# Hybrid encoder layer on one core: the Fourier group's fold as first work, raw column weights in memory of their own, residual squares to SBUF, output weights split before a scan unit

## The chip, the core and the metric

The kernel runs on one core of a Trainium2 chip. The core has a matrix engine (PE; its weight loads are listed as PEld), a vector engine (DVE), a scalar engine (ACT), a small general engine (POOL) and a sequencer that here issues nearly all DMA transfers (SP). Each takes its instructions in order from its own queue and waits on semaphores. SBUF is the working memory of 128 partitions; PSUM holds eight banks of 512 fp32 a partition, into which PE writes. The metric is the device time of one execution, in microseconds; the time before is the median of three runs.

## The reference: what is computed

One layer of a trunk over 2048 tokens of 1024 channels. A modulated RMS norm is followed by one input projection, whose columns go to a Fourier group and to a two-way gated linear attention group; both are gated, joined, projected back and added to the residual stream, and a last RMS norm follows.

```python
h = rmsnorm(x, norm_g[layer]) * (1.0 + scale[:, None, :]) + shift[:, None, :]
proj = h @ w_in[layer]
u_f, z_f, q, k, v, r, gf_low, gb_low = jnp.split(proj, pts, axis=-1)
y_f = fourier_mix(u_f, w_fmap[layer]) * jax.nn.silu(z_f)
y_g = gla_mix(q, k, v, gf_low, gb_low, w_af[layer], b_af[layer],
              w_ab[layer], b_ab[layer], gla_norm_g[layer]) * jax.nn.silu(r)
y = jnp.concatenate([y_f, y_g], axis=-1) @ w_out[layer]
x = x + gate[:, None, :] * y
...
# fourier_mix
spec = jnp.fft.fft2(ug, axes=(1, 3), norm="ortho").real
y = jnp.einsum("blgc,gcd->blgd", spec, w_map.astype(jnp.float32))
```

## The kernel before

**Halves and blocks.** The tokens are worked in two halves, the second (m = 1) first. For each half the normed input A is held in 14 SBUF tiles: seven combinations of quarter blocks, each as a high and a low part, since products are made of three matmuls (high by high, high by low, low by high), and a projection block of 2 x 2 quarters is made with seven products instead of eight. Column blocks (`block_col`, L272: q, k, z, r) take 84 matmuls of 512 columns; token blocks (`block_tok`, L315: u, v) take twice four times that in narrower ones. The weights of a block pass through `b_prep` for the second half: a raw tile is loaded, differences are formed on DVE (L228 to L236), ACT makes the high part (L48) and DVE the low one (L49), and the seven results, tiles named B in a pool of six, are stored for the first half, which only loads them.

**The start.** x of the second half is loaded (`x_tiles`), squared on ACT and summed on DVE (`x_rstd`: L138, L141, L142), summed over partitions on PE (L145), and the root is made on POOL (L148) and spread by PE (L164). Meanwhile PE makes the modulation rows from `ada` tiles, two tiles a row (L923 to L930). Then DVE scales x (L171) and A is built (L181 to L193, L48, L49).

**After the first value block.** `do_v(1, A, 0)` is followed by the loads of the fold and of the residual gate's weights, by `do_v(1, A, 1)`, by the fold, the gate row and the rows' squares. The fold multiplies the channel DFT table with each group's map: 32 matmul statements into eight PSUM tiles (L396), each copied by ACT to a staging tile (L399) and stored to `fold_d`. Its input tiles lie in the gate's pool. Then the token pools are closed and two column pools opened in their place, staging and `colraw`, the one raw tile for column weights; `do_q(1, A, 8)` is the first to use it.

**Scan and output.** A scan unit is one pair of heads over 256 tokens, done in two steps: a preparation on ACT and DVE (L493 to L543), scores (L553, L554), a product with the state (L603), a transpose (L564) and the state's update (L56, L575). Units are written beside projection blocks, which fill PE while ACT and DVE prepare. For the first half the last four column blocks, r, stand behind one unit each; then the first four pairs of output weights are loaded and split (`split_out_weights`, L1043, L1044) into the A tiles, which come free as the last block proceeds. The other four units stand beside Fourier parts of the output product (`out_fourier`, L843, 48 statements each), and the remaining splits are spread between them. At the end, for each 128 tokens, `out_fwd` adds the product to x and squares the sum for the norm (L872), with its unneeded result going back into the PSUM tile of the product.

**What sets the order.** The program text gives an order with priorities, and a list scheduler, which plans with a model of the machine, decides the queue of every engine. So a change of the text moves rows on all engines.

Of the kernel before, what the change touches and what calls it, by code (L numbers as in the profile page):

```python
# [12 lines left out]
F32 = mybir.dt.float32  # L13
F32R = mybir.dt.float32r
BF16 = mybir.dt.bfloat16
# [6 lines left out]
P = 128  # L22
# [13 lines left out]
def hybrid_kernel(ctx, tc, i, out):  # L36
# [4 lines left out]
    def load(dst, src):  # L41
        nc.sync.dma_start(dst, src)
# [336 lines left out]
            store(vd_[tt:tt + 2, :, cs].rearrange("a p n -> p a n"), v)  # L379
        block_tok(A, weights("tok", 2 + j, m), WC, 1, emit)  # L380

    def fold_load(gg, gw):
        fin = gw.tile([P, 2048], F32, tag="fold", name="fold_in", bufs=2)
        tabs = fin[:, 0:1024].rearrange("p (k w) -> p k w", k=2)
        wf = fin[:, 1024:2048].rearrange("p (g k d) -> p g k d", g=2, k=2)
        load(tabs, i["chtab"].rearrange("k p w -> p k w"))
        load(wf, i["w_fmap"][2 * gg:2 * gg + 2].rearrange("g (k p) d -> p g k d", p=P))
        return tabs, wf

    def fold(gg, tabs, wf):  # L390
        for g in range(2):
            for w in range(2):
                ps = pj_tile()
                for ct in range(2):
                    for k in range(2):
                        T.matmul(ps[:, ct * 256:(ct + 1) * 256], tabs[:, k, w * 256 + ct * P:w * 256 + (ct + 1) * P],  # L396
                                 wf[:, g, k, :], start=(k == 0), stop=(k == 1))
                s = stage_tile()
                S.activation(s[:, 0:512], ps[:], AF.Copy)  # L399
                store(fd_[:, 2 * gg + g, w * 512:(w + 1) * 512], s[:, 0:512])  # L400

    def gate_sums(gw):
        acc = gw.tile([P, D], F32, name="gacc")
# [392 lines left out]
    def tail_fwd(sc, os_, sr):  # L796
        for hp in range(2):
            o = os_[hp]
            ss = op.tile([P, 2], F32, tag="ss", name="ss", bufs=4)
            for h in range(2):  # L800
                jk = op.tile([P, 256], BF16, tag="jk", name="jk", bufs=1)
                S.activation(jk[:], o[:, h * 256:(h + 1) * 256], AF.Square, accum_out=ss[:, h:h + 1])  # L802
            r = rstd(ss[:], 2, 256)
            for h in range(2):
                V.tensor_scalar(o[:, h * 256:(h + 1) * 256], o[:, h * 256:(h + 1) * 256], r[:, h:h + 1], None,
                                ALU.mult)
            tp = pg.tile([P, 4, P], F32, tag="tr", name="otr")
            for c in range(4):
                T.transpose(tp[:, c, :], o[:, c * P:(c + 1) * P], ident[:])  # L809
            y = sr[:, 4 * hp:4 * hp + 4, :]  # L810
            V.tensor_tensor(y, tp[:], y, ALU.mult)
        return sr
# [50 lines left out]
    def out_fwd(sc, ys, yf):  # L863
# [5 lines left out]

        def residual(n):  # L870
            xs_ = gated_add(x, ps, n)
            S.activation(ps[n][:], xs_, AF.Square, accum_out=ss[:, n:n + 1])  # L872

        if sc == 15:
            for k in range(4):
# [20 lines left out]
    with ExitStack() as st_stack:  # L896
# [13 lines left out]
        def load_ada(j):  # L910
# [2 lines left out]
                load(t[h], i["w_ada"][j][:, 4 * h:4 * h + 4, :])  # L913
            return t

        xs = x_tiles(1)
        rb = x_rstd(xs)
        A = a_tiles()
        for j in range(KT):
# [17 lines left out]

    xstack.close()
    do_v(1, A, 0)
    gw = pool(glate, "gate")  # L940
    folds = [fold_load(g, gw) for g in range(2)]
    acc = gate_sums(gw)
    do_v(1, A, 1)
    for g in range(2):
        fold(g, *folds[g])
    gate_row(acc, gw)
    rows_rms(gw)
    tok.close()
    n_st = 2
    sp = pool(col, "stagec", side="right")  # L950
    cr = pool(col, "colraw", side="right")
    do_q(1, A, 8, qd_)
    do_q(1, A, 10, kd_)
    glate.close()
# [12 lines left out]
    for hp in range(2):  # L967
        store(sst_[hp], st_b[hp][:].rearrange("p h t -> p (h t)"))
    gstack.close()
    col.close()  # L970
    sp = pool(tok, "stage3", side="right")
    tk = pool(tok, "tokraw3", side="right")
# [93 lines left out]
            gts[blk] = gates(blk)  # L1066
        scan_back(blk, hp, gts[blk], st_b)

    for blk in range(12, 16):
        next_unit()  # L1070
        do_r(0, A, blk)
    for j in range(4):
        split_out_weights(j, st_w)
    ph2.close()
# [106 lines left out]
```

## Time and profile before

| what | us |
|---|---|
| median of three runs | 1695.24 |
| lowest, highest | 1693.71, 1698.9 |
| the profiled execution | 1696.42 |
| its span, from the first to the last instruction | 1694.6 |
| DMA moved in the span | 400.42 MB, mean 236 GB/s |

A page of the profile gives busy times of the engines, the span in 40 slices, the DMA queues, the chain of work that ended last, and groups of instructions by line with the idle time ahead of them. A row of the timeline has the start, the length, the engine (SPq is SP's issuing of transfers), the line, the operation, what it writes and reads, how many were merged, and in brackets how long the engine had been idle and what released it. A row of the stretches has the borders and length, for each engine the busy time and count, then the mean granted clock of PE, the DMA engines' busy share and the rate. An fp32 matmul statement stands in the profile as two records.

### The profile page before, as it was taken

The page shows a single profiled execution, that of the slowest core. Times are in us where ns is not written, and L with a number is a line of the kernel's source. Part 1 is how long each engine was busy: PE and PEld are TensorE (multiplying, and loading weights), DVE is VectorE, ACT ScalarE, POOL GpSimd, SP SyncE. Part 2 cuts the span into 40 slices and gives each one's busy share as a digit, 9 for nine tenths or more (in the row PEclk, how much of TensorE's full clock was granted, in tenths as well). Part 3 has the DMA queues.
Part 4 walks back from the last instruction along what each step waited for, and adds up shares of the span by engine and source line. Part 5 has one row for each costly group of instructions (what it writes and reads, how often), then busy time and mean ns, then how long its engine had stood idle before and what let it go on. Part 6 is the DMA issues. An engine that isn't in the chain of part 4 may idle for free. (4 is left out here: it accounts for less than half of the span.)

```text
span 1694.6 us, 25167 instructions
## 1 busy us (share of the span) xinstructions
PE 1580.2 (93%) x9012; PEld 1358.2 (80%) x9012; DVE 1174.1 (69%) x2424; ACT 692.9 (41%) x1294; POOL 60.8 (4%) x118
## 2 busy tenths in 40 slices
PE   5899899999989999999999999978999999999997
PEld 2599678778889988989998887857887778778876
DVE  4964588877578444887887646678876865777673
ACT  3723244433244201313232407677543543454452
POOL 0000000000000000000000000000010111111110
PEclk9999999999999999999999999978999999999999
DMA  8498888778977689879897688866654333343432
GB/s 293 161 389 325 294 317 288 278 281 307 327 286 284 226 267 363 277 234 319 252 337 220 224 289 277 286 225 226 222 165 145 122 130 119 115 137 127 149 94 75
DMA packets 220332, 400.42 MB, mean 236 GB/s; under 512 B 19504, under 2 KB 121776, under 8 KB 216624
## 3 DMA queue, kind: packets, MB, share of 16 engines
q1 hardware_dynamic: 220064, 398.56, 68.6%
q8 instruction: 71, 1.16, 0.3%
q14 instruction: 53, 0.43, 0.1%
q10 hardware_dynamic: 144, 0.26, 0.0%
HBM read 238.13 MB, written 160.63 MB: 235 GB/s over the span
## 5 line engine op out<-in xcount | busy, mean ns | idle before, releaser
L272 PE MATMUL pj<-A_hi,B 128*128 128x512 f32 x1344 | 437.0, 400 | 16.6 <-ACT B L48 12.8
L315 PE MATMUL pj<-B,A_hi 128*128 128x264 f32 (+1 forms) x1792 | 336.0, 288 | 17.5 <-DMA B<-btok_d 6.6
L272 PEld LDWEIGHTS pj<-A_hi,B 128*128 128x128 f32 x1344 | 251.2, 188 | 77.8 <-ACT B L48 15.1
L315 PEld LDWEIGHTS pj<-B,A_hi 128*128 128x128 f32 x1792 | 283.5, 193 | 22.1 <-DVE B L49 6.0
L272 PE MATMUL pj<-A_lo,B 128*128 128x512 f32 x672 | 267.4, 398 | 0.0
L315 PE MATMUL pj<-B,A_lo 128*128 128x264 f32 (+1 forms) x896 | 255.3, 287 | 2.3 <-DVE A_lo L49 2.3
L315 PEld LDWEIGHTS pj<-B,A_lo 128*128 128x128 f32 x896 | 173.0, 194 | 2.5 <-DVE A_lo L49 2.5
L272 PEld LDWEIGHTS pj<-A_lo,B 128*128 128x128 f32 x672 | 126.8, 189 | 27.1
L843 PE MATMUL po<-wo_hi,fhi 128*128 128x512 f32 x256 | 108.5, 424 | 12.1 <-ACT po L872 6.2
L843 PE MATMUL po<-wo_hi,ghi 128*128 128x512 f32 x256 | 103.9, 406 | 1.9 <-ACT ghi L48 1.9
L843 PE MATMUL po<-wo_lo,fhi 128*128 128x512 f32 x256 | 105.2, 411 | 0.0
L843 PE MATMUL po<-wo_lo,ghi 128*128 128x512 f32 x256 | 103.4, 404 | 0.0
L843 PE MATMUL po<-wo_hi,flo 128*128 128x512 f32 x256 | 95.2, 414 | 0.2 <-DVE flo L49 0.2
L843 PE MATMUL po<-wo_hi,glo 128*128 128x512 f32 x256 | 88.6, 410 | 2.6 <-DVE glo L49 2.6
L276 DVE TENSOR_TENSOR u<-u,pj 128x512 f32<-128x512 f32 x96 | 65.4, 681 | 26.0 <-PE pj L272 23.7
L583 ACT ACTIVATE vh<-v 128x512 fp32r<-128x512 f32 x64 | 40.1, 626 | 99.0 <-PE upd L56 87.2
L48 ACT ACTIVATE B<-raw 128x512 fp32r<-128x512 f32 x72 | 42.8, 624 | 91.2 <-DMA raw<-in_w_in 42.0
L575 DVE SCALAR_TENSOR_TENSOR state<-state,sm,upd 128x256 f32<-128x256 f32 x112 | 48.8, 474 | 37.0 <-PE upd L56 36.8
L320 DVE TENSOR_TENSOR u<-u,pj 128x264 f32<-128x264 f32 (+1 forms) x96 | 48.9, 515 | 35.8 <-PE pj L315 35.7
L843 PEld LDWEIGHTS po<-wo_hi,fhi 128*128 128x128 f32 x256 | 50.7, 198 | 25.8 <-ACT po L872 8.2
L56 PE MATMUL mapA<-PQ,wm 128*128 128x256 f32 x480 | 65.8, 287 | 1.8 <-ACT PQ L48 1.4
L56 PEld LDWEIGHTS mapA<-PQ,wm 128*128 128x128 f32 x480 | 62.4, 194 | 3.7 <-ACT PQ L48 1.9
(221 smaller groups left out, 3042.9 us busy)
## 6 DMA issues: line engine op xcount, KB each, us to landing
bcol_d<-B SPq DMA_DIRECT2D x84, 512.0 KB, 4.1
B<-bcol_d SPq DMA_DIRECT2D x84, 512.0 KB, 4.9
v<-v_d SPq DMA_DIRECT2D x64, 256.0 KB, 3.5
btok_d<-B SPq DMA_DIRECT2D x28, 528.0 KB, 9.2
B<-btok_d SPq DMA_DIRECT2D x28, 528.0 KB, 6.7
btok_d<-B SPq DMA_DIRECT2D x28, 512.0 KB, 4.5
B<-btok_d SPq DMA_DIRECT2D x28, 512.0 KB, 5.9
raw<-in_w_in SPq DMA_DIRECT2D x12, 1024.0 KB, 7.6
```

The lines of the kernel that those rows point to most:

```text
L48: S.activation(hi, src, AF.Copy)
L56: T.matmul(ps, a, b, start=(k == 0), stop=(k == n - 1))
L272: T.matmul(ps[:], B[k][0][:, bq, p, :], A[k][aq][:, p, :], start=(p == 0 and q == 0), stop=(p == 3 and q == 2))
L276: V.tensor_tensor(o, a, ps[:], ALU.add)
L315: T.matmul(ps[:, j, :], A[k][aq][:, p, t * P:(t + 1) * P], B[k][p // 2][:, bq, p % 2, :], start=(p == 0 and q == 0), stop=(p == 3 and q == 2))
L320: V.tensor_tensor(o[:, cut], a[:, cut], ps, ALU.add)
L575: V.scalar_tensor_tensor(state[:, h, :], state[:, h, :], dec[:, g:g + 1], up_[:, h, :], ALU.mult, ALU.add)
L583: S.activation(vh[:], v[:], AF.Copy)
L843: T.matmul(ps[n][:], a, wo[j0 + j][q][:, cs], start=(first and a is yh and q == 0), stop=(last and a is yl))
```

## The change

Four things are changed.

- The fold becomes the first work of the program: its tables and all four groups' maps are loaded ahead of x, into two tiles of the token weights' raw pool, and its matmuls are written ahead of `x_rstd`.
- `colraw` is opened right behind the first value block, in memory of its own on the left side, and closed after the scan's first part.
- The residual squares of `out_fwd` go to a scratch tile in SBUF, bf16, which the normalisation in `tail_fwd` shares (its tile grows from 256 to 512 columns).
- The fourth scan unit of the first half leaves the loop over the r blocks: three units stand with three r blocks, the fourth r block and the split of the first output weights follow, and then five units (instead of four) stand beside Fourier parts of the output.

```diff
--- before.py
+++ after.py
@@ -379,16 +379,15 @@
             store(vd_[tt:tt + 2, :, cs].rearrange("a p n -> p a n"), v)
         block_tok(A, weights("tok", 2 + j, m), WC, 1, emit)
 
-    def fold_load(gg, gw):
-        fin = gw.tile([P, 2048], F32, tag="fold", name="fold_in", bufs=2)
-        tabs = fin[:, 0:1024].rearrange("p (k w) -> p k w", k=2)
-        wf = fin[:, 1024:2048].rearrange("p (g k d) -> p g k d", g=2, k=2)
+    def fold_load():
+        tabs = tk.tile([P, 2 * BW], F32, tag="traw", name="fold_t", bufs=2)[:, 0:1024].rearrange("p (k w) -> p k w", k=2)
         load(tabs, i["chtab"].rearrange("k p w -> p k w"))
-        load(wf, i["w_fmap"][2 * gg:2 * gg + 2].rearrange("g (k p) d -> p g k d", p=P))
+        wf = tk.tile([P, 2 * BW], F32, tag="traw", name="fold_w", bufs=2)[:, 0:2048].rearrange("p (g k d) -> p g k d", g=4, k=2)
+        load(wf, i["w_fmap"].rearrange("g (k p) d -> p g k d", p=P))
         return tabs, wf
 
-    def fold(gg, tabs, wf):
-        for g in range(2):
+    def fold(tabs, wf):
+        for g in range(NG):
             for w in range(2):
                 ps = pj_tile()
                 for ct in range(2):
@@ -397,7 +396,7 @@
                                  wf[:, g, k, :], start=(k == 0), stop=(k == 1))
                 s = stage_tile()
                 S.activation(s[:, 0:512], ps[:], AF.Copy)
-                store(fd_[:, 2 * gg + g, w * 512:(w + 1) * 512], s[:, 0:512])
+                store(fd_[:, g, w * 512:(w + 1) * 512], s[:, 0:512])
 
     def gate_sums(gw):
         acc = gw.tile([P, D], F32, name="gacc")
@@ -798,8 +797,8 @@
             o = os_[hp]
             ss = op.tile([P, 2], F32, tag="ss", name="ss", bufs=4)
             for h in range(2):
-                jk = op.tile([P, 256], BF16, tag="jk", name="jk", bufs=1)
-                S.activation(jk[:], o[:, h * 256:(h + 1) * 256], AF.Square, accum_out=ss[:, h:h + 1])
+                jk = op.tile([P, 512], BF16, tag="jk", name="jk", bufs=1)
+                S.activation(jk[:, 0:256], o[:, h * 256:(h + 1) * 256], AF.Square, accum_out=ss[:, h:h + 1])
             r = rstd(ss[:], 2, 256)
             for h in range(2):
                 V.tensor_scalar(o[:, h * 256:(h + 1) * 256], o[:, h * 256:(h + 1) * 256], r[:, h:h + 1], None,
@@ -869,7 +868,8 @@
 
         def residual(n):
             xs_ = gated_add(x, ps, n)
-            S.activation(ps[n][:], xs_, AF.Square, accum_out=ss[:, n:n + 1])
+            jk = op.tile([P, 512], BF16, tag="jk", name="jk", bufs=1)
+            S.activation(jk[:], xs_, AF.Square, accum_out=ss[:, n:n + 1])
 
         if sc == 15:
             for k in range(4):
@@ -913,7 +913,9 @@
                 load(t[h], i["w_ada"][j][:, 4 * h:4 * h + 4, :])
             return t
 
+        folds = fold_load()
         xs = x_tiles(1)
+        fold(*folds)
         rb = x_rstd(xs)
         A = a_tiles()
         for j in range(KT):
@@ -937,18 +939,16 @@
 
     xstack.close()
     do_v(1, A, 0)
+    craw = ExitStack()
+    cr = pool(craw, "colraw")
     gw = pool(glate, "gate")
-    folds = [fold_load(g, gw) for g in range(2)]
     acc = gate_sums(gw)
     do_v(1, A, 1)
-    for g in range(2):
-        fold(g, *folds[g])
     gate_row(acc, gw)
     rows_rms(gw)
     tok.close()
     n_st = 2
     sp = pool(col, "stagec", side="right")
-    cr = pool(col, "colraw", side="right")
     do_q(1, A, 8, qd_)
     do_q(1, A, 10, kd_)
     glate.close()
@@ -967,6 +967,7 @@
     for hp in range(2):
         store(sst_[hp], st_b[hp][:].rearrange("p h t -> p (h t)"))
     gstack.close()
+    craw.close()
     col.close()
     sp = pool(tok, "stage3", side="right")
     tk = pool(tok, "tokraw3", side="right")
@@ -1066,9 +1067,10 @@
             gts[blk] = gates(blk)
         scan_back(blk, hp, gts[blk], st_b)
 
-    for blk in range(12, 16):
+    for blk in range(12, 15):
         next_unit()
         do_r(0, A, blk)
+    do_r(0, A, 15)
     for j in range(4):
         split_out_weights(j, st_w)
     ph2.close()
```

The first place is the program's start. PE's queue before (`row` is the modulation row, `ss` the sum of squares, `rbp` the spread root, `cps` the row turned to columns):

```order
L923 MATMUL row<-ada,vecs 1x256 x4
L145 MATMUL ss<-ones,rb 128x1 x8
L923 MATMUL row<-ada,vecs 1x256 x4
L164 MATMUL rbp<-ident,ms 128x128 x4
L928 MATMUL cps<-ones,rs 128x1 x2
L923 MATMUL row<-ada,vecs 1x256 x8
L164 MATMUL rbp<-ident,ms 128x128 x4
```

and now:

```order
L395 MATMUL pj<-fold_w,fold_t 128x256 x32
L925 MATMUL row<-ada,vecs 1x256 x2
L145 MATMUL ss<-ones,rb 128x1 x8
L925 MATMUL row<-ada,vecs 1x256 x6
L164 MATMUL rbp<-ident,ms 128x128 x4
L930 MATMUL cps<-ones,rs 128x1 x2
L925 MATMUL row<-ada,vecs 1x256 x8
```

All 32 fold statements stand ahead of PE's first row, and the sum of squares behind two row statements instead of four. SP's queue at the same place before, behind the small constants:

```order
L42 DMA xs<-in_xT 128x2x512 x8
L42 DMA ada<-in_w_ada 128x1024 x6
L42 DMA traw<-in_w_v 128x2112 x2
L42 DMA ada<-in_w_ada 128x1024 x10
L45 DMA btok_d<-B 128x1056 x8
```

and now:

```order
L42 DMA fold_t<-in_chtab 128x2x512
L42 DMA fold_w<-in_w_fmap 128x8x256
L42 DMA xs<-in_xT 128x2x512 x8
L42 DMA ada<-in_w_ada 128x1024 x6
L45 DMA fold_d<-st 128x512 x4
L42 DMA traw<-in_w_v 128x2112 x2
L42 DMA ada<-in_w_ada 128x1024
L45 DMA fold_d<-st 128x512
L42 DMA ada<-in_w_ada 128x1024
L45 DMA fold_d<-st 128x512 x3
L42 DMA ada<-in_w_ada 128x1024 x8
```

The two fold loads stand ahead of x; the stores of the fold's results stand among the `ada` loads, and the loads of the value weights (`traw`) behind four of them.

The second place is the change from the second value block to the first column block. ACT before (`st` is the fold's staging tile, `gater` the gate row, `row` a row of x for its squares, `raw` the raw column weights):

```order
L156 ACTIVATE row,ssl<-row 128x1024
L48 ACTIVATE B<-traw 128x528 x2
L156 ACTIVATE row,ssl<-row 128x1024
L399 ACTIVATE st<-pj 128x512 x2
L156 ACTIVATE row,ssl<-row 128x1024
L399 ACTIVATE st<-pj 128x512 x6
L416 ACTIVATE gater<-pj 128x512 x2
L48 ACTIVATE B<-raw 128x512
L48 ACTIVATE wabhi<-wabs 128x512
```

and now:

```order
L156 ACTIVATE row,ssl<-row 128x1024
L48 ACTIVATE B<-traw 128x528 x2
L156 ACTIVATE row,ssl<-row 128x1024
L48 ACTIVATE B<-traw 128x528
L48 ACTIVATE B<-raw 128x512 x3
L48 ACTIVATE B<-t_1579 128x512
L48 ACTIVATE B<-raw 128x512
L415 ACTIVATE gater<-pj 128x512 x2
L48 ACTIVATE B<-raw 128x512 x2
L278 ACTIVATE p_1607<-pj 128x512
```

The fold's copies are gone from there, and five of the seven splits of the first column block stand ahead of the gate row. SP during the first value block now (`p_607` and `p_638` are its first results):

```order
L42 DMA gacc<-in_b_gate 128x1024
L42 DMA gwa<-in_w_gate 128x1024 x2
L45 DMA btok_d<-B 128x1056
L42 DMA row<-in_x 128x1024 x2
L45 DMA v_d<-p_607 128x2x264
L42 DMA raw<-in_w_in 128x2048
L42 DMA gwa<-in_w_gate 128x1024
L45 DMA v_d<-p_638 128x2x264
```

The load of the raw column weights stands there; before, it stood behind the store of the gate row:

```order
L45 DMA v_d<-u_1089 128x2x264
L45 DMA v_d<-u_1057 128x2x264
L45 DMA v_d<-u_1088 128x2x264
L45 DMA fold_d<-st 128x512 x8
L45 DMA gate_d<-gater 128x1024
L42 DMA raw<-in_w_in 128x2048
L42 DMA sel<-in_sel 128x2
```

The third place is ACT's queue from the second half of the third output weights (before: the first half of the fourth) to the first split of the Fourier results, `fhi`. Before:

```order
L1043 ACTIVATE wo_hi_11002<-wot 128x1024
L606 ACTIVATE obs<-ob 128x512
L499 ACT_TABLE_LOAD
L499 ACTIVATE pa<-pa 128x512
L356 ACT_TABLE_LOAD
L356 ACTIVATE u_10862<-u_10862 128x512
L583 ACTIVATE vh<-v 128x512
L500 ACT_TABLE_LOAD
L500 ACTIVATE pa<-pa 128x512
L1043 ACTIVATE wo_hi_11002<-wot 128x1024
L477 ACTIVATE gt<-gf 128x256
L48 ACTIVATE fhi<-y 128x512 x2
```

and now:

```order
L1044 ACTIVATE wo_hi_10885<-wot 128x1024
L596 ACTIVATE sb<-sc 128x256
L498 ACT_TABLE_LOAD
L498 ACTIVATE pa<-pa 128x512
L1044 ACTIVATE wo_hi_10895<-wot 128x1024
L48 ACTIVATE kth<-ktr 128x256
L499 ACT_TABLE_LOAD
L499 ACTIVATE pa<-pa 128x512
L1044 ACTIVATE wo_hi_10895<-wot 128x1024
L605 ACTIVATE obs<-ob 128x512
L476 ACTIVATE gt<-gf 128x256
L48 ACTIVATE fhi<-y 128x512 x2
```

Between the splits now stand the fourth unit's scores (`sb`), its second transpose (`kth`) and its product with the state (`obs`), and the last r block's gating (`u`, with a table load of its own) has left this piece.

## The prediction

> **What bounds the kernel now.** I read the page's busy times first, then the mean clock and busy time of stretches cut at stage borders, then the timeline where PE is not full.
>
> ```profile
> span 1694.6 us, 25167 instructions
> PE 1580.2 (93%) x9012; PEld 1358.2 (80%) x9012; DVE 1174.1 (69%) x2424; ACT 692.9 (41%) x1294; POOL 60.8 (4%) x118
> core 0: us, PE busy (x) PEld busy (x) DVE busy (x) ACT busy (x) POOL busy (x), PEclk, DMA share, GB/s
> 0.00:18.10 18.10, 0.00 (x0) 0.00 (x1) 7.98 (x16) 10.10 (x18) 0.19 (x4) 1.00 0.82 294
> 36.60:85.00 48.40, 40.20 (x221) 24.94 (x220) 46.79 (x84) 32.96 (x56) 0.00 (x0) 0.93 0.47 165
> 85.00:154.30 69.30, 69.30 (x574) 69.30 (x573) 46.44 (x88) 20.47 (x36) 0.00 (x0) 1.00 1.03 396
> 154.30:177.80 23.50, 15.84 (x72) 12.88 (x70) 2.32 (x7) 7.72 (x14) 1.65 (x1) 0.92 0.59 210
> 177.80:181.00 3.20, 3.20 (x8) 2.49 (x9) 3.16 (x8) 1.46 (x3) 0.00 (x0) 0.52 0.41 166
> 181.00:260.00 79.00, 78.00 (x358) 63.04 (x357) 60.44 (x112) 31.88 (x62) 0.00 (x0) 1.00 0.88 318
> 1088.20:1113.30 25.10, 25.10 (x128) 21.05 (x127) 15.51 (x28) 16.60 (x24) 0.00 (x0) 1.00 0.77 245
> 1113.30:1129.60 16.30, 4.58 (x14) 3.30 (x13) 12.45 (x18) 14.53 (x21) 0.00 (x0) 0.59 0.81 289
> 1129.60:1163.00 33.40, 28.21 (x129) 22.73 (x129) 29.10 (x58) 24.88 (x40) 0.00 (x0) 0.86 0.64 213
> 1163.00:1220.00 57.00, 56.96 (x279) 47.49 (x279) 50.28 (x98) 37.60 (x60) 0.00 (x0) 0.96 0.70 232
> ```
>
> PE is busy for 93% of the span, so the end moves only with PE's work, its holes, or its clock. The stretches show the holes. PE does nothing for the first 18.1 us. From 36.6 to 85 us DVE is full (46.79 of 48.40), so a delay there passes through. From 85 to 154.3 PE is full. Then come 23.5 us with the fold and a hole, and 3.2 us at half clock. The next thin place is 1113 to 1163. PE is also at a mean of 0.97 of its clock, because holes are followed by half clock.
>
> **Part 1: the fold leaves the middle, and the raw weights come early.**
>
> ```profile
> 154.41 13.98 PE L396 MATMUL pj<-fold_in 128*128 128x256 f32 x64
> 168.22 1.88 PE L415 MATMUL pj<-gacc,ones 128*128 128x512 f32 x4
> 177.77 0.80 PE L272 MATMUL pj<-A_hi,B 128*128 128x512 f32 x1 [7.67 <-ACT B L48]
> 171.31 0.33 SPq L42 DMA_DIRECT2D raw<-in_w_in  x1
> 177.09 0.63 ACT L48 ACTIVATE B<-raw 128x512 fp32r<-128x512 f32 x1 [6.35 <-DMA raw<-in_w_in]
> ```
>
> Between 154.41 and 177.77 PE folds for 13.98 us (32 matmul statements, 64 records of fp32), makes the gate row (1.88) and waits 7.67 us for the first split of raw column weights, whose load was issued only at 171.31. Changed, the fold is gone from there, and the order shows that load among the first value block's, with five of the seven splits ahead of the gate row's copies on ACT. The gate row stays: 23.36 - 1.88 = 21.5 us saved. The half clock of 177.8:181.0 went with the hole: 3.2 us at 0.52 instead of 1.00 is 1.5 us. **Sum -23.0.** Late next would be the second raw load, one buffer still: it waits for the seventh split, which waits for a B buffer, free after the block's first step; against a block of 84 matmuls at 78.00 / 358 = 0.218 us, 18 us, it is hidden; the cost if that cover goes is the old wait of 6.35 us. The memset that had waited for the gate row's store now stands behind that block's first four additions, so it should not hold them up.
>
> **Part 2: the fold at the start.**
>
> ```profile
> 6.96 0.63 ACT L138 ACTIVATE rb<-xs 128x512 f32<-128x512 f32 x1 [4.26 <-DMA xs<-in_xT]
> 17.46 1.90 DVE L142 TENSOR_TENSOR rb<-rb,sq 128x512 f32<-128x512 f32 x3 [0.22 <-ACT sq L141]
> 18.13 3.57 PE L923 MATMUL row<-ada,vecs 128*1 128x256 f32 x8 [18.13 <-DMA ada<-in_w_ada]
> 21.63 3.57 PE L145 MATMUL ss<-ones,rb 128*128 128x1 f32 x16
> 25.13 3.57 PE L923 MATMUL row<-ada,vecs 128*1 128x256 f32 x8
> 25.49 1.65 POOL L148 TENSOR_TENSOR ms<-ms,mhalf 128x8 f32<-128x8 f32 x1 [25.06 <-DVE ms L147]
> 31.19 3.62 PE L923 MATMUL row<-ada,vecs 128*1 128x256 f32 x16
> 34.73 1.16 PE L164 MATMUL rbp<-ident,ms 128*128 128x128 f32 x8
> 36.66 9.16 DVE L171 TENSOR_TENSOR xs<-xs,rb 128x1024 f32<-128x1024 f32 x8
> ```
>
> Ahead of x on SP's queue now stand 0.5 and 1.0 MB, 1.57 million bytes, at 294 GB/s 5.3 us. The sum of squares, ready at 17.46 + 1.90 = 19.4, comes at 24.7. The first arrival, at 6.96, is now the tables'; the map weights follow 3.6 us later, so PE folds from 10.5. At full clock it needs 14 us; the clock is first half: eight row matmuls take 3.57 us at 18.13 and sixteen take 3.62 at 31.19. I allow 5 us of half clock (behind the middle's hole it was 3.2), costing 2.5: the fold ends at 27.0. Two row statements later, at 28, the sums' matmuls (L145) start, 6.4 us after their 21.63. From there to the scaling of x took 36.66 - 21.63 = 15.0 us, largely at half clock. At full clock it is about 11: sums 1.8 (half of 3.57), the root 1.65 with hand-overs 2.1, two spreads of 1.16, row and column work 4.2, copies 0.7. Scaling starts at 39.2, 2.5 us later, and the DVE-full stretch passes it on. Add 0.7 us for the one subtraction that slips behind the scaling on DVE, and some for the queues: ACT's fifth to eighth evictions need a staging buffer whose store stands behind six table loads on SP, and the later ada loads stand behind those evictions' stores. I take **+4.0**. The ends: -2, if the transfers hide and the clock helps; +18.7, if it stays half: 64 records at 2 x 13.98 / 64 = 0.437 us end at 38.5, then rows 1.8 and the old 15.0.
>
> By the Trainium skill, "TensorE: Matmul & The Clock Gate", Part 1, about 3.4 us of sustained activity release the clock, whatever runs. The row at 18.13 speaks against "whatever": PE ran on from there with single-column work, and the row at 25.13, again 3.57 for eight, was still at half. By the rule the term would be some 1 us smaller; by that row, were the fold the same kind of work, some 4 us larger.
>
> **Part 3: squares to SBUF.**
>
> ```profile
> L872 ACT ACTIVATE po<-xr x32: 575/583/604, 1263.0 to 1688.1; 128x512 f32<-128x512 f32 x32
> PE po L843 <- ACT po L872: 6.2, 5, 2.1
> L141 ACT ACTIVATE sq<-xs x14: 612/613/630, 7.5 to 17.9; 128x512 f32<-128x512 f32 x14
> ```
>
> The square no longer holds the bank that the next products want; DVE's addition frees it. PE waited five times for it, 6.2 us. Each wait shortens by ACT's 0.58 us and its hand-over, perhaps half of it, and some half clock with it: **-3.0**, ends 0 and -8. The square itself costs 613 instead of 583 ns, 1 us in 32, on an ACT with idle time; the new wider scratch has one buffer, but only ACT writes it, in order.
>
> By the Trainium skill, "ScalarE: Activation LUTs", Step-by-step: what each stage is for, a PSUM destination is the quicker one for ScalarE. The two rows agree by 30 ns; obeying it would save ACT 1 us and return the 3 us of waits.
>
> **Part 4: weights ahead of the fourth unit.**
>
> ```profile
> 1103.32 1.06 ACT L1043 ACTIVATE wo_hi<-wot 128x1024 fp32r<-128x1024 f32 x1 [4.07 <-DMA wot<-in_w_out]
> 1117.63 2.08 PE L603 MATMUL ob<-state,Q 128*128 128x256 f32 x4 [4.11 <-DVE state L575]
> 1126.06 0.63 ACT L500 ACTIVATE pa<-pa 128x512 f32<-128x512 f32 x1
> 1127.56 0.77 PE L493 MATMUL lg<-gt,wab 128*128 128x256 f32 x2 [6.33 <-DVE pa L501]
> 1129.61 0.80 PE L843 MATMUL po<-wo_hi,fhi 128*128 128x512 f32 x1 [1.28 <-ACT fhi L48]
> 1150.11 1.95 PE L603 MATMUL ob<-state,Q 128*128 128x256 f32 x4 [2.15 <-DVE state L575]
> 1333.50 6.56 PE po L843 x28
> L499 ACT ACT_TABLE_LOAD x1 | 1.3, 1283 | 0.0
> wot<-in_w_out SPq DMA_DIRECT2D x16, 512.0 KB, 4.5
> ```
>
> After the last r block PE idles 16.3 - 4.6 = 11.7 us and then 5.2 of 33.4, and half clock costs about 7 more (2.3 of the 4.58, and 0.14 x 33.4): 24 us in all. The eight splits (1.06 us each on ACT) cannot come sooner: their buffers free with the block's steps and each load takes 4.5 us. In the new order the last r block runs nearly alone, 18 us and 1.5 of the third unit's matmuls; the fifth weight load needs its last buffer, is issued at about 20 and lands at 24.5. Behind it stand on ACT four splits (4.2 us), two table loads (2.6), a dozen small operations of the fourth unit of up to 0.63 (some 6) and the first split of yf (0.6). So the products start some 38 to 39 us after the last r block's first matmul (at 1088.2, by counting 84 back), where they took 1129.6 - 1088.2 = 41.4: 2 us won. The rest comes behind: 48 products stand unbroken under the fifth unit's preparation, where two units ran bare from 1144 to 1163, the row at 1150.11 among them. Of that stretch's 5.2 + 4.7 I take half, 5, and give 2 back for the block that then fails the first forward part as cover: **-5 in all**. Ends: -16 and +8.
>
> **Sum.** The profiled execution took 1696.42 us. -23.0 + 4.0 - 3.0 - 5.0 = -27.0: 1669.4. The median of three is 1695.24, 1.2 lower: **1668**.
>
> **The rivals.** *Transfers become the bound (0.13).* From 85 to 260 us the rows sum to 27.4 + 4.9 + 0.5 + 25.1 = 58 million bytes; less 4.2 of the fold, 53.8 must pass in 152 us: 354 GB/s. For it: that is near the 396 of the full stretch. Against: 396 was held for 69 us. If only 318 is sustained, 17 us come back: 1685. *The fold costs as much ahead as it freed (0.08)*, at the upper end of part 2, by half clock and ACT's queue: 1683. *Too little to cover the units (0.05), the slower side.* Place: from the weights to the first forward part. The 24 us there fell on some 2.5 units, 9.6 each; if all five lose that, 24 us more, and the block missing from the forward part most of its 48 x 6.56 / 28 = 11.2, say 8: 1696.4 - 23 + 4 - 3 + 32 = 1706. It decides from where a unit's ACT and DVE chain outlasts its 48 products and its own matmuls. Against: 1163:1220 has two such units with PE full. *The weights place gives nearly all (0.10)*: -16 instead of -5, 1657. That the raw load doesn't move is ruled out by the order.
>
> **How the numbers follow.** Forecast 0.62 (1660 to 1680), rivals as given, 0.02 for the rest. The range 1655 to 1687 leaves out the slow rival and tails on both sides. A measurement tells 0.3%, 5 us. Faster 0.91, within 0.05, slower 0.04.
>
> **What would show it.** Right: no hole between the gate row and the first column block; scaling of x near 39; no wait of PE for the residual squares of L872; PE idle for under 9 us behind the last r block. Wrong: half clock through the whole fold, splits of raw waiting for their load, or PE thin past 1163.

## The result and the profile after

| | before | after |
|---|---|---|
| median, us | 1694.47 (1691.16 to 1698.9, 4 runs) | 1670.55 (1666.69 to 1671.36, 4 runs) |
| the profiled execution, us | 1696.42 | 1670.82 |
| its span, us | 1694.6 | 1669.0 |

The ratio is 0.9853, with a 95% interval of 0.9825 to 0.988: by it 25 us faster, where 27 were forecast. The sum came out; most of its terms did not. The page of the kernel after, its span and busy times:

```profile
span 1669.0 us, 25145 instructions
PE 1570.0 (94%) x9012; PEld 1352.1 (81%) x9012; DVE 1176.3 (70%) x2424; ACT 695.7 (42%) x1295; POOL 60.4 (4%) x118
```

To see where the time came from, both executions are cut at the same nine events of PE: first and last matmul of the two value blocks, first of the first column block, first token block after the scan, first column block of the first half, last matmul of the last r block, first product with Fourier results, first product with attention results, last matmul. The stretches of before (columns as in the prediction; the stretch from 1113.30 is shown there):

```profile
0.00:54.60 54.60, 34.26 (x149) 16.86 (x149) 28.29 (x51) 22.50 (x37) 1.84 (x5) 1.00 0.75 272
54.60:154.60 100.00, 94.02 (x718) 88.05 (x718) 76.70 (x143) 43.34 (x78) 0.00 (x0) 0.97 0.83 319
154.60:177.80 23.20, 15.54 (x69) 12.57 (x68) 2.32 (x7) 7.72 (x14) 1.65 (x1) 0.92 0.59 208
177.80:472.20 294.40, 285.95 (x1359) 234.18 (x1360) 223.10 (x420) 110.69 (x219) 0.00 (x0) 0.99 0.85 302
472.20:898.10 425.90, 405.27 (x2952) 385.00 (x2951) 304.45 (x708) 124.59 (x215) 0.00 (x0) 0.97 0.82 280
898.10:1113.30 215.20, 212.76 (x1110) 178.85 (x1108) 127.64 (x261) 93.16 (x154) 0.00 (x0) 1.00 0.79 261
...
1129.60:1240.10 110.50, 104.55 (x505) 86.00 (x506) 92.22 (x182) 68.47 (x115) 1.78 (x4) 0.94 0.65 213
1240.10:1685.40 445.30, 423.23 (x2148) 353.40 (x2148) 303.56 (x636) 206.61 (x441) 54.64 (x105) 0.97 0.39 124
```

And of after:

```profile
0.00:56.40 56.40, 44.02 (x212) 27.22 (x212) 28.47 (x51) 26.39 (x45) 1.83 (x5) 1.00 0.90 329
56.40:159.40 103.00, 96.20 (x718) 89.14 (x718) 81.60 (x152) 47.60 (x85) 1.65 (x1) 0.97 0.83 321
159.40:160.60 1.20, 1.20 (x5) 0.48 (x4) 1.08 (x3) 0.30 (x2) 0.00 (x0) 1.00 0.66 252
160.60:446.30 285.70, 281.94 (x1353) 232.79 (x1351) 221.81 (x417) 111.25 (x218) 0.00 (x0) 0.99 0.83 299
446.30:879.90 433.60, 407.82 (x2975) 386.75 (x2974) 307.74 (x715) 124.33 (x218) 0.00 (x0) 0.98 0.83 282
879.90:1091.70 211.80, 208.34 (x1068) 174.37 (x1067) 123.09 (x251) 91.20 (x148) 0.00 (x0) 1.00 0.78 257
1091.70:1109.30 17.60, 9.19 (x43) 7.40 (x41) 11.67 (x16) 14.39 (x22) 0.00 (x0) 0.71 0.88 305
1109.30:1218.30 109.00, 101.48 (x508) 84.43 (x509) 94.31 (x186) 68.98 (x116) 1.22 (x2) 0.95 0.68 224
1218.30:1659.40 441.10, 419.80 (x2147) 349.52 (x2145) 303.16 (x636) 209.83 (x445) 54.74 (x107) 0.98 0.39 125
```

The second column of each row is the stage's length. Differences, after less before:

| stage | us | forecast |
|---|---|---|
| start, to the first value block | +1.8 | +4.0 |
| the two value blocks | +3.0 | 0 |
| gate row and hole | -22.0 | -21.5 |
| column blocks beside the scan | -8.7 | -1.5 |
| token blocks and Fourier stage | +7.7 | 0 |
| column blocks of the first half | -3.4 | together -8 |
| last r block to the first product | +1.3 | |
| Fourier products beside units | -1.5 | |
| the forward part | -4.2 | |
| behind the last matmul | +0.4 | 0 |

The borders are events, so work that the planner moves over a border counts as lost on one side and as won on the other. PE has 2975 records in the Fourier stage now where it had 2952, and 1068 in the stage behind it where it had 1110, so not all of the +7.7 and of the -3.4 is lost or won.

At the start PE now folds before it does anything else (timeline of after):

```profile
10.08 15.86 PE L395 MATMUL pj<-fold_w,fold_t 128*128 128x256 f32 x64 [10.08 <-DMA fold_w<-in_w_fmap]
...
26.82 1.95 PE L145 MATMUL ss<-ones,rb 128*128 128x1 f32 x16
...
38.47 2.35 DVE L171 TENSOR_TENSOR xs<-xs,rb 128x1024 f32<-128x1024 f32 x2
```

The fold begins at 10.08 (10.5 forecast), the sums at 26.82 (28), and the scaling of x at 38.47 (39.2).

### The profile page after: what moved, and what is told of

Same layout as the page of the kernel before. It is cut to its first block, busy times and chain, and to the rows that moved or that the text cites. A ratio compares the mean times of both kernels' runs of the same rounds, so it can differ in the third digit from the quotient of the medians.

```text
span 1669.0 us, 25145 instructions
## 1 busy us (share of the span) xinstructions
PE 1570.0 (94%) x9012; PEld 1352.1 (81%) x9012; DVE 1176.3 (70%) x2424; ACT 695.7 (42%) x1295; POOL 60.4 (4%) x118
## 5 line engine op out<-in xcount | busy, mean ns | idle before, releaser
L842 PEld LDWEIGHTS po<-wo_hi,fhi 128*128 128x128 f32 x256 | 50.6, 197 | 24.4 <-ACT fhi L48 9.5
L784 POOL TENSOR_SCALAR rstd<-ss 128x2 f32<-128x2 f32 (+1 forms) x48 | 15.8, 330 | 1365.6 <-ACT jk L801 1364.2
```

What stands on the lines that cost most here:

```text
L784: G.tensor_scalar(r[:, 0:n], ss, 1.0 / width, EPS, ALU.mult, ALU.add)
L842: T.matmul(ps[n][:], a, wo[j0 + j][q][:, cs], start=(first and a is yh and q == 0), stop=(last and a is yl))
```

## The experiments

The stretches above are single executions, and the planner moves rows far from an edit, so each part was undone alone in the changed kernel, two were done alone in the kernel before, and then variants were run for the prices that stayed in dispute. A ratio is to the kernel before on the same chip, in brackets its 95% interval; 0.001 is 1.7 us. A difference between two kernels is that of their ratios, and its "either way" the root of the summed squares of their half intervals. Stage lengths are from each run's own profile, cut at the same events.

### Undo one part at a time

**Squares back to PSUM.**

```diff
-            jk = op.tile([P, 512], BF16, tag="jk", name="jk", bufs=1)
-            S.activation(jk[:], xs_, AF.Square, accum_out=ss[:, n:n + 1])
+            S.activation(ps[n][:], xs_, AF.Square, accum_out=ss[:, n:n + 1])
```

> The changed kernel (median 1670.55 us) with one part undone: the residual squares go back into the PSUM tile of the product. Theory 1 (the prediction's part 3: PE waited 6.2 us for that square, and half of it with some half clock is won): about 3 us slower, 1673.5, with waits of PE for the square of about 6 us back in the output part. Rival (in the changed kernel PE waits 3.6 us for DVE's addition where it had waited for the square, so the next thing was already late): within 1 us, 1670.5, waits for the square come back but those for the addition go.

1677.24 us, 0.9895 [0.9875, 0.9916]: the squares are worth 7 us here, 6 either way. PE's order is that of the changed kernel up to the forward part, which takes 448.1 instead of 441.1 us. The waits of PE there:

```profile
PE po L842 <- ACT po L871: 6.1, 6, 2.1
```

The old wait is back in its old size (us, times, longest). In the changed kernel PE had waited there for DVE's addition instead:

```profile
PE po L842 <- DVE xr L848: 3.6, 3, 1.5
```

These waits are gone in the undo, as the rival said, so of the 6.1 us only 2.5 are more waiting at the bank itself. The rival's time (within 1 us) is not what was measured. The forward part of this kernel:

```profile
1218.80:1666.90 448.10, 423.43 (x2147) 352.52 (x2145) 304.62 (x636) 207.98 (x444) 55.32 (x107) 0.97 0.39 123
```

Against the stretch of after, PE idles 24.7 us instead of 21.3 and is busy for 3.6 us more, for the same 2147 records.

**The units' old place.**

```diff
-    for blk in range(12, 15):
+    for blk in range(12, 16):
         next_unit()
         do_r(0, A, blk)
-    do_r(0, A, 15)
```

> The changed kernel (median 1670.55 us) with one part undone: four scan units stand in the loop over the r blocks again and the output weights follow it. Theory 1 (the prediction's part 4): 5 us slower, 1675.5, with PE idle 11.7 and 5.2 us behind the last r block as before. Rival (the trace of the changed kernel shows the products starting 17.6 us behind the last r block's end, where it was 16.3, with 8.4 us idle there; the place gave nothing and was only moved): within 2 us of 1670.5. A second rival, that the move gave all that the output part won: 8 us slower, 1678.5.

1669.78 us, 0.9858 [0.9833, 0.9884]: no difference that can be told (0.8 us, 6 either way): nearest to the first rival, though the 5 us of theory 1 are not excluded. The hole behind the last r block is 15.8 us (16.3 before, 17.6 after); PE idles for 14.8 of it, where it idles for 8.4 after, but the forward part is 433, 8 shorter than after.

**The raw weights' old place**, with the fold still first.

```diff
-    craw = ExitStack()
-    cr = pool(craw, "colraw")
...
     sp = pool(col, "stagec", side="right")
+    cr = pool(col, "colraw", side="right")
...
-    craw.close()
```

> The changed kernel (median 1670.55 us) with one part undone: the raw column weights' pool is opened in the place of the token pools again; the fold stays first. Theory 1 (the prediction: the early load removes a wait of 7.7 us and its half clock, 1.5, and costs nothing): 9.2 us slower, 1679.7, all of it between the gate row and the first column block. Theory 2 (read from the two traces: the early load also makes PE wait about 2.5 us in the second value block, where the DMA engines are full, and it lets the splits of all later raw loads run ahead, which takes 5 us of waits out of the scan's stage): +9.2 + 5 - 3, 11 us slower, 1681.7, with no wait of PE in the value block at 119 and the waits for column splits in the scan's stage back at about 5 us. Rival (without the fold the value block ends later, so the hole is covered): within 2 us.

1683.43 us, 0.9925 [0.9906, 0.9944]: 12 us slower. The value blocks take 100.0 again, the column blocks beside the scan 294.7, and the hole is back (timeline of this kernel):

```profile
156.98 1.88 PE L414 MATMUL pj<-gacc,ones 128*128 128x512 f32 x4
166.35 0.80 PE L272 MATMUL pj<-A_hi,B 128*128 128x512 f32 x1 [7.49 <-ACT B L48]
```

PE's waits for splits, from the end of the value blocks to the end of the scan's stage, in this kernel (us, times, longest), and then in the changed one:

```profile
PE pj L272 <- ACT B L48: 12.5, 4, 7.5
```

```profile
PE pj L272 <- ACT B L48: 2.8, 2, 1.9
```

Theory 2 holds in all three of its signs: 7.5 us of hole, the other 5.0 us of waits for splits in the blocks behind it (2.8 after), and no loss in the value blocks. But the stage from the token blocks to the first half's column blocks is 426.3 here and 433.6 after: in these two executions 7 us of what the early load won were given back there.

**The fold's old place**, with its inputs in the token weights' raw tiles, so that the raw column weights keep their memory.

```diff
-        folds = fold_load()
         xs = x_tiles(1)
-        fold(*folds)
...
     do_v(1, A, 1)
+    fold(*fold_load())
```

> The changed kernel (median 1670.55 us) with one part undone: the fold runs behind the second value block again; its inputs lie in the token weights' raw tiles, which come free in that block, and the raw column weights keep memory of their own. Theory 1 (the prediction's part 2: ahead it costs 1.8 us by the trace, 4 by forecast, behind it takes 14 us of PE): 12 us slower, 1682.7, with scaling of x back at 36.7. Theory 2 (its 1.5 MB then fall into the full transfers of the second value block): 14 to 18 us slower, with waits for transfers ahead of the fold. Rival (the fold costs as much ahead as it frees): within 3 us.

1683.08 us, 0.9926 [0.9904, 0.9948]: 12 us slower, theory 1's size, with a transfer in front of the fold as theory 2 said:

```profile
159.46 15.74 PE L395 MATMUL pj<-fold_w,fold_t 128*128 128x256 f32 x64 [2.76 <-DMA fold_w<-in_w_fmap]
```

### One part alone

**The squares alone**: the edit to `residual` and the wider `jk`, on the kernel before.

> The kernel before with one part alone: the residual squares to SBUF. The prediction's part 3 gave 3 us: ratio 0.998. The undo of this part cost 6 to 7 us, and 5 us between the first column block of the first half and the end: 0.996 if that holds with the old place of the output weights. Read from the same stage of four profiles (before 787 us, squares undone 785, weights place undone 774, changed kernel 780), the squares are worth 13 us where the weights stand at their old place: 0.992.

1675.89 us, 0.9886 [0.9862, 0.991]: **19 us** (4 either way) of the 25, by the smallest edit. Even the largest of the three expectations was too small. PE's order is the same as before until some 20 us into the forward part, and that part is where most of it lies; its stretch:

```profile
1243.10:1667.03 423.93, 413.72 (x2148) 345.94 (x2148) 301.49 (x636) 209.34 (x442) 54.34 (x105) 1.00 0.42 130
```

445.3 became 423.9. Idle time fell from 445.30 - 423.23 = 22.1 to 10.2 us, and busy time for the same 2148 records by 9.5, with the clock at 1.00 instead of 0.97. So each microsecond of PE's idle time that went took 0.8 of half clock with it (9.5 for 11.9). In the undo above it was 1.1 (3.6 for 3.4).

Only 6.2 of the 11.9 us of idle time had been waits for the square, by the row in the prediction. The largest of the others was the first product of a scan unit (`lg`), which waited for DVE; before, and then here:

```profile
PE lg L493 <- DVE pa L501: 5.1, 2, 3.7
```

```profile
PE lg L493 <- DVE pa L501: 0.3, 1, 0.3
```

So the bank's own wait, counted whole and with its half clock, makes some 11 of the 19 us (6.2 x 1.8, an estimate from these rows). Whether the rest followed from it or from the order that the planner made of the forward part is not shown.

**The units alone**: the loop's edit, on the kernel before.

> The kernel before with one part alone: the fourth scan unit behind the output weights. The prediction's part 4: 5 us faster, ratio 0.997. By the undo (the old place was 1 us faster by the medians, within their spread): 1.000. By the stage from the first column block of the first half to the end (785 with squares undone against 787 before): 2 us faster, 0.9985. What the trace should show if the place gives nothing: PE's idle time behind the last r block goes from 17 us to under 10, and as much comes back behind the next units.

1708.05 us, 1.0072 [1.0045, 1.0099]: 12 us **slower**. The hole behind the last r block and what follows:

```profile
1111.90:1127.50 15.60, 0.77 (x2) 0.50 (x2) 11.24 (x16) 14.87 (x20) 0.00 (x0) 0.57 0.60 209
1127.50:1244.00 116.50, 107.47 (x550) 90.26 (x551) 101.55 (x202) 75.12 (x129) 1.78 (x4) 0.95 0.68 224
1244.00:1699.00 455.00, 429.55 (x2146) 356.76 (x2145) 303.44 (x634) 207.38 (x440) 51.48 (x105) 0.96 0.38 120
```

The hole has not shrunk (15.6, was 16.3; PE is busy for 0.77 of it), the Fourier products take 6 more than before and the forward part 9.7 more.

### Is it the bank?

The undo gave 7 us, the part alone 19. So the bank was held again, with the square left in SBUF:

```diff
             S.activation(jk[:], xs_, AF.Square, accum_out=ss[:, n:n + 1])
+            S.activation(ps[n][:, 0:1], xs_[:, 0:1], AF.Copy)
```

> The kernel with the squares in SBUF alone (1675.9 us, ratio 0.9886), and behind each square one more copy by ACT of a single column into the PSUM tile of the product, so that the bank is held for ACT again while the square itself stays in SBUF. It adds 32 copies of a column, some 0.2 us each, 6 us of ACT, which has idle time. Up to the forward part PE's order is that of before. Theory 1 (the bank held for ACT is what cost): PE's waits for ACT on the product's bank come back, the forward part takes 440 to 447 us instead of 424, ratio 0.997 to 1.000. Rival (the planner made another, luckier order of the forward part; the hold itself is worth its 6 us of waits at most): 430 us at most, ratio 0.989 to 0.993.

1688.65 us, 0.9965 [0.995, 0.9979]: 13 of the 19 us are gone again (5 either way). Its forward part:

```profile
1243.50:1678.90 435.40, 419.57 (x2148) 350.54 (x2148) 302.81 (x636) 212.10 (x472) 55.23 (x105) 0.98 0.40 127
```

PE's wait for the bank there, and the added copy by its line (durations in ns, least, median and most):

```profile
PE po L843 <- ACT po L874: 4.1, 3, 2.6
```

```profile
L874 ACT ACTIVATE po<-xr x32: 148/154/175, 1263.9 to 1682.0; 128x1 f32<-128x1 f32 x32
```

The result lies between the two expectations, nearer to theory 1: the interval reaches its 0.997, though the stretch (435) stops short of its 440. It is not a test of a short hold. In all three places where PE waited, a square stood directly ahead of the copy on ACT, so that the bank was held for both; the first of them (ACT, then PE):

```profile
1315.08 0.61 ACT L873 ACTIVATE jk<-xr 128x512 bf16<-128x512 f32 x1
1315.60 0.19 ACT L873 ACTIVATION_READ_ACCUMULATOR jk<-xr 128x1 f32 x1
1315.69 0.15 ACT L874 ACTIVATE po<-xr 128x1 f32<-128x1 f32 x1
1315.90 0.79 PE L843 MATMUL po<-wo_hi,fhi 128*128 128x512 f32 x1 [0.49 <-ACT po L874]
```

The bank's share is not isolated by it either, since the copies also add 32 x 0.154 = 5 us of ACT and the planner orders the forward part anew in each of these kernels. How much of the remaining 6 us, and of the difference between 7 and 19, is order stays open.

### Is it transfers, and is it the order?

**Rows' squares written later.**

```diff
-    rows_rms(gw)
...
     do_q(1, A, 10, kd_)
+    rows_rms(gw)
```

> The changed kernel (1670.55 us) with the squares of the rows of x, 4 MB of loads, written behind the second column block instead of beside the gate row. If PE's wait in the second value block comes from full transfers (theory 1), the two value blocks take 100 us again instead of 103 with the raw column load still early, 3 us faster, 1667.5. Rival (the early splits themselves stand in the way on ACT): still 103. The order that the planner makes for the Fourier stage is a third one here, neither that of before nor that of the changed kernel; theory 2 is that the changed kernel gave 8 us back in the stage from the first token block after the scan to the first column block of the first half (434 us, and 426 before and with the raw memory undone) by its order alone: then this stage may come out anywhere between, and not at 434 by necessity; rival to it: the raw memory itself costs 8 us there, then it is 434 again.

1675.73 us, 0.9887 [0.9863, 0.991]: no gain (6 us slower, 6 either way). But the value blocks take 100.1 again, with the raw load as early as ever. SP's issue of the second value weights and the split that waits for the second of them, after and here:

```profile
101.50 0.33 SPq L42 DMA_DIRECT2D traw<-in_w_v  x1
107.19 0.33 SPq L42 DMA_DIRECT2D traw<-in_w_v  x1
...
119.43 1.18 ACT L48 ACTIVATE B<-traw 128x528 fp32r<-128x528 f32 x2 [3.50 <-DMA traw<-in_w_v]
```

```profile
101.31 0.33 SPq L42 DMA_DIRECT2D traw<-in_w_v  x1
104.68 0.33 SPq L42 DMA_DIRECT2D traw<-in_w_v  x1
...
117.17 1.18 ACT L48 ACTIVATE B<-traw 128x528 fp32r<-128x528 f32 x2 [3.32 <-DMA traw<-in_w_v]
```

The planner still pulled the rows' loads into the blocks; only one of them now stands behind the second `traw` instead of ahead of it, which goes out 2.5 us sooner. So, as far as this pair shows, the 3 us were the place of one load in a full queue. The Fourier stage, in the third order, takes 427.5: theory 2. So it is not the early raw load itself that costs there, but the order that the planner makes around it; what in its model turns the order was not tried.

The size of that cost is less sure. The kernel before and three others have the same order of PE's work in this stage, the changed kernel and four others a second one, three kernels a third; the two left (426.3 with the raw weights' old place, 434.8 with the fold's) have orders of their own. The lengths, one execution each:

| PE's order in the Fourier stage | us | mean |
|---|---|---|
| that of before | 425.9, 429.7, 430.1, 431.6 | 429.3 |
| that of the changed kernel | 431.8, 433.6, 434.4, 436.7, 438.1 | 434.9 |
| the third | 423.2, 427.5, 427.5 | 426.1 |

So one execution of the same order can be off by 6 us, and between the means 5.6 are left of the 7.7. Of the 7.7, 2.6 are busy time (407.82 against 405.27): PE has 23 records more in the stage, 10 from the stage ahead of it and 13 from the stage behind.

What was won up to the first half's column blocks (6 us) was lost behind them: from there to the last matmul 790.6 instead of 779.5.

**The fold's loads behind x.**

```diff
-        folds = fold_load()
         xs = x_tiles(1)
-        fold(*folds)
+        folds = fold_load()
         rb = x_rstd(xs)
+        fold(*folds)
```

> The changed kernel (1670.55 us) with the fold's loads behind those of x and its matmuls written behind the sum of squares. Theory 1: x is scaled at 36.7 again instead of 38.5, and the value block starts 1.8 us sooner: 1668.7, or less, if the fold warms PE for the rows. Rival: the fold's loads then delay those of the modulation rows by 5 us, and the scaling comes no sooner: 1670 to 1674. The Fourier stage has the same third order as the kernel with the rows moved: by theory 2 (its order alone decides) both show the same length there; by the rival 434 us.

1679.76 us, 0.9905 [0.988, 0.9929]: 9 us slower than the changed kernel (6 either way), which neither expectation named. Scaling starts at 37.2, near theory 1, but the fold then stands ahead of the modulation rows, whose first is at 40.3. The value blocks begin at 67.1 instead of 56.4, and their last matmul comes at 165.9 instead of 159.4. Fold first is the better start. (The profiled execution took 1673.06 us, 6.7 less than the median.) The Fourier stage, in the third order again, takes 423.2.

### Does the weights' move lack cover?

```diff
-    ahead = [0, 2, 5, 8, 11, 15]
+    ahead = [0, 2, 5, 8, 11, 13, 15]
```

In the changed kernel:

> The changed kernel (1670.55 us, ratio 0.9853) with a seventh Fourier part (tokens of part 13) worked ahead of the forward parts, so that two of them stand beside the first forward part again, as before the change. Theory 1 (the weights' move took a cover from the first forward part, and that is why the old place is no worse): 5 to 8 us faster, ratio 0.981 to 0.982, PE's idle time in the first 60 us behind the fifth unit falls. Rival (the loss is spread over the forward part by its order): within 2 us, and the extra store and load of x change nothing.

1667.54 us, 0.9842 [0.9821, 0.9864]: 1.9 us faster, 6 either way, so nearest to the rival, without excluding theory 1's 5. The same with the units at their old place:

> The changed kernel with the output weights at their old place (1669.8 us, ratio 0.9858) and seven Fourier parts worked ahead instead of six. Theory 1 (missing cover belongs to the weights' move): here the cover was there, so within 2 us of 0.9858. Rival (a part more ahead helps in either place, since the later forward part that keeps only its own products is shorter): 3 to 8 us faster, 0.981 to 0.984.

1676.46 us, 0.9896 [0.9877, 0.9916]: 6 us slower (5 either way), which neither expectation named. And the units' old place in the kernel with the rows' squares later:

> The kernel with the squares of the rows written later (1675.7 us, ratio 0.9887) and the output weights at their old place. By the stages of the profiles: everything to the first column block of the first half as there (872 us), then 771 us as in the two kernels with squares in SBUF and the old place (774 and 767) instead of 791: 1653 us, ratio 0.975. Prediction's part 4 (the new place is worth 5 us): 1681, ratio 0.992. Rival (no difference by the place, as the medians of the undo said): 0.9887.

1670.52 us, 0.9857 [0.9835, 0.988]. So there are four pairs that differ in the units' place alone:

| on | new place | old place |
|---|---|---|
| the kernel before | 1.0072 | 1 |
| the changed kernel | 0.9853 | 0.9858 |
| with the rows later | 0.9887 | 0.9857 |
| with seven parts ahead | 0.9842 | 0.9896 |

The seventh part gives nothing that can be told in the new place and costs 6 us in the old one, so missing cover is not shown. The new place is 12 us worse, equal, 5 worse (within its error) and 9 better. For the last run the stages of other kernels had promised 1653 us: adding up stages of different kernels fails. The fastest, 1667.54 us, is the new place with seven parts, not distinguishable from the changed kernel.

## Why the prediction was right, and where it was not

**Part 1, -23.** The mechanism is right: the undo costs 12 us for the raw weights and 12 for the fold. -22.0 was measured at the place itself, and no hole is left between the gate row and the column block. Two sizes were off. "Late next would be the second raw load ... it is hidden": splits of later raw loads had been late in the old order. They now run further ahead in the scan's stage; by the two stretches PE idles 294.40 - 285.95 = 8.5 us there before and 3.8 after, and with 4.0 us less of busy time that is 8.7, where only 1.5 of half clock was forecast. Of the 4.0, 1.3 is work that moved into the next stage (the ten records that came to it from ahead). And the early load was costed at nothing in the value blocks, where the DMA engines are full: 3 us, because a load that PE needs was issued later. This is the rival of full transfers in small, 3 instead of 17.

**Part 2, +4.** Against this profile of before +1.8. But the start is not the same in every execution. These rows are from the squares alone, whose start is that of before:

```profile
18.13 3.29 PE L924 MATMUL row<-ada,vecs 128*1 128x256 f32 x8 [18.13 <-DMA ada<-in_w_ada]
21.34 1.95 PE L145 MATMUL ss<-ones,rb 128*128 128x1 f32 x16
23.22 1.89 PE L924 MATMUL row<-ada,vecs 128*1 128x256 f32 x8
```

The same eight row matmuls that took 3.57 us at 25.13 in the profiled execution of before take 1.89 at 23.22 here. Five profiles with the old start begin their value blocks at 50.3, 50.6, 54.6, 54.8 and 54.9 us, mean 53.0; the eight with the fold first at 56.4 to 57.3, mean 57.0. So the term is +4.0 between the means, but +6.6 against the two early starts and +2.2 against the three late ones. The prediction worked it out from an execution of the late kind, for which +4.0 was 2 us too much; that it meets the mean is luck.

The traces also list when the full clock was granted. With the fold first it came 3.7 to 5.5 us after PE's first matmul, in all eight executions. With the old start it came after 2.9 and 3.6 us in the two early ones and after 12.0 to 12.6 in the three late ones. (The stretches' clock column reads 1.00 there only because nothing is listed ahead of the first grant.) The fold's 64 records took 15.86 us, 1.9 more than their 13.98 in the middle of the kernel before, which is what 3.7 us at half clock cost. By the Trainium skill, "TensorE: Matmul & The Clock Gate", Part 1, some 3.4 us of sustained activity release the clock. The grants after 2.9 to 5.5 us are near that, those after 12 us are not. The prediction laid the row that was still at half clock to the kind of work. That alone does not decide it, since the same rows came to full clock within 3 us in the squares alone. Whether the kind of work has a part (late in three of five executions with the rows first, in none of eight with the fold first), and what else delays the grant, stays open.

**Part 3, -3.** The mechanism was right, no wait for the square is left, and the square itself costs 0.631 us instead of 0.583. The term that was mis-sized is "perhaps half of it, and some half clock with it". Alone, the wait of 6.2 us went whole but for 0.3 us for DVE's addition, with nearly as much again of half clock, and some 8 us more came that are not told apart: 19 us, of which 13 went when the bank was held again. In the changed kernel, where DVE's addition was late for 3.6 us, it was 7, just inside the end of -8.

**Part 4, -5.** The walk nearly held: the products start 1109.3 - 1069.1 = 40.2 us after the last r block's first matmul, counted as before (38 to 39 forecast, 41.4 before), and PE idles 17.60 - 9.19 = 8.4 us there. But "the rest comes behind" failed. With units alone it came to +12; in four pairs the sign changes. The slower rival (too little to cover the units) had the place right, though not the price: alone, the hole and the Fourier products take 5 us more, where its sum had 24, and the forward part 10, where it had 8.

**Not in the sum at all:** +7.7 in the Fourier stage (5.6 between the means, part of it work that moved there), from an order made anew by an edit hundreds of us earlier. It and the 3 us in the value blocks took back what the scan's stage gave beyond forecast. The stages up to the first half's column blocks come to -18.2 (-19 forecast), those behind to -7.8 (-8): errors that cancelled, so the total is right in part by luck. Nor do the parts add up: the four undos cost 7, 1, 12 and 12 us, together some 32, where the whole change gave 25 and the squares alone 19.

## What to carry to other kernels

Where a bank is held for a result that nobody reads, write that result elsewhere, even if the work costs a little more (here 0.631 us instead of 0.583). Count the wait whole, take off what PE will then wait for the engine that frees the bank instead, and add half clock (here 0.8 to 1.1 us for each 1). Where a planner orders the rows, an edit's price has a spread of its own, here -9 to +12 us for one move of a unit in four kernels, so undo each part alone, and do it alone, before crediting any of them. A load made early in a stretch with full transfers is not free: look at what PE-critical load is issued behind it.

## What the runs showed of the hardware

The time at which PE comes to full clock at the start differs between executions with the same rows: the sums of L145 took 3.57 us in the profiled execution of before and 1.95 in that of the squares alone, and the value blocks then began 4.3 us apart. With the fold first, the full clock came within 5.5 us in all eight executions. Later stages differ too: the Fourier stage took 425.9 to 431.6 us in four executions with the same order of PE's work. A difference of a few us between two single profiles is not yet a difference between two kernels.

A short wait of PE costs more than its length. In the forward part no wait listed for the bank was longer than 2.6 us, and each microsecond of idle time came with 0.8 to 1.1 us more of busy time for the same records, in three pairs of executions (before and the squares alone: 11.9 and 9.5; the undo and after: 3.4 and 3.6; the bank held again and the squares alone: 5.6 and 5.9). The mean clock of these stretches is 0.97 to 0.98 in the longer and 0.98 to 1.00 in the shorter kernel of each pair.
